# One transformer step on one core: everything behind the projections done for tokens 0-511, then for 512-1023

## The chip, the core and the metric

The kernel runs on one core of one Trainium2 chip. The core has five engines that run beside each other, each with its own queue of instructions taken in order: TensorE (PE, with its weight loads as PEld), VectorE (DVE), ScalarE (ACT), GpSimd (POOL) and SyncE (SP), which issues the DMAs. Waits between queues go by semaphores. The metric is the device time of one execution in microseconds.

## What is computed

One layer for 1024 new tokens of one sequence (D = 1024, the prompt) and 32 tokens of a second one that has 256 cached positions (the sample). Inputs and outputs are fp32.

```python
h = rms_norm(x, norm1_g) * (1 + sc1) + sh1
z = h @ w_in                                   # 1024 x 2884
q, k, v, qi, ki, wi, u, vg = jnp.split(z, SPLIT_POINTS, axis=-1)
...
score = jnp.einsum('bqhs,bqh->bqs', jax.nn.relu(s), w_idx)
score = jnp.where(mask[None], score, -jnp.inf)
top_val, top_idx = lax.top_k(score, topk)      # topk = 256, for the sample 72
...
p = jax.nn.softmax(logits, axis=-1)            # over the selected keys, 8 heads of 64
...
y = jnp.concatenate([attn.reshape(B, T, WIDTH_A), gm], axis=-1) @ w_out
x = x + g1 * y
h2 = rms_norm(x, norm2_g) * (1 + sc2) + sh2
x = x + g2 * (jnp.square(jax.nn.relu(h2 @ w_ff1)) @ w_ff2)   # 4096 hidden features
```

A query of the block b of 128 tokens sees at most the keys 0 to 128(b+1)-1. So blocks 0 and 1 need no selection, and a late block has more scores to search and more keys to attend to than an early one. `gm` is the gated unit, mixed within 128 positions.

## The kernel before

Every fp32 operand of a large product is split into two parts (a rounded one, and the difference), and a product is three passes (`PASSES`). A split of weights is a cast on ScalarE and a subtraction on VectorE or GpSimd (lines 183-184 for w_in, 756-757 for the rest).

**Front** (to about 475 us). Six groups of columns of z go through `zgroup` (line 303 has the matmul): first the indexer's columns, whose scores `score[b]` follow block by block, then q, the gated unit, k, v, each with its norms and rotations on VectorE and GpSimd. `ada` multiplies the conditioning vector. In between stand the searches of `find_top`: 31 bits of the k-th largest score are found one by one. On VectorE a bit is a trial value from GpSimd (line 551), one count for each block of the search (line 519), and two small operations (lines 554 and 555). On ScalarE a bit is a sum of signs (line 545) and two small operations on GpSimd (546 and 547). Search `tb` takes blocks 2 and 3, `tc` blocks 5, 4 and NB (the sample) on VectorE, `ta` block 7 and `td` block 6 on ScalarE. The four are generators, stepped round-robin:

```python
    while searches:
        searches = [f for f in searches if next(f, "end") is None]
```

This stands ahead of the last group (v) in the code; the framework's scheduler lists the instructions of each engine by a simulated time, so the steps spread over the whole front.

**Attention** (475 to 629 us), `attention(b)` for blocks 0, 2, 1, 3, 4, 5, NB, 6, 7. The queries are transposed (`qst`, line 351) and split (`qs`, 353-354). For each of 8 heads: scores of the keys into `lgp` (663), their masked minimum (664), Exp (665), scaling by the reciprocal on GpSimd (668), transposes `ppt` (675) and products with v (`pv`, 688). The keys stay in SBUF as `kst`. PSUM has 3 banks for lgp, 2 for ppt, 2 for pv, 1 for qst.

**Projection and perceptron** (629 to 1494 us). x, h2 and the hidden features lie with features on the partitions and all 1056 tokens (sample behind the prompt) in three chunks of 352 columns (`CW`). Weights are loaded and split once and stay while the three chunks pass. `wo` (812) adds to x; `norm2(c)` sums squares by a matmul with ones (783) and spreads the reciprocal root by another (789), among the wo and first f1 products of other chunks; `ff1` (831) and `ff2` (868) alternate over 16 groups of 256 hidden features, `gated` adds to x (749), `emit` transposes x back and stores.

## Time and profile before

| | us |
|---|---|
| three runs, median | 1496.52 |
| three runs, from and to | 1495.24 and 1497.37 |
| the profiled execution, first to last instruction | 1494.1 |
| front, to the first qst of attention | 474.8 |
| attention | 154 |
| projection with norm 2 | 112 |
| perceptron and end | 753 |

The profiled execution is shown by its span; the device times of the runs lie a little above it. The mean granted TensorE clock was 0.973 of full speed. A row of a view gives start and length or busy time in us; "idle before" is the time in which the engine did nothing ahead of a group's instructions, followed by what ended it.

### The profile page before, as it was taken

How to read it: one execution, taken by the hardware profiler on the slowest of the kernel's cores; microseconds unless marked ns; L12 is line 12 of the kernel's file. 1: busy time of each engine (PE TensorE's matmuls, PEld its weight loads, DVE VectorE, ACT ScalarE, POOL GpSimd, SP SyncE). 2: the span in 40 equal slices, each digit the busy share in tenths (PEclk: the TensorE clock that was granted, in tenths of full speed). 3: DMA queues.
4: the chain of work that ended last, by engine and by line, in shares of the span. 5: the costliest groups of instructions: out<-in, count | busy, mean ns of one | idle time of the engine just before them, and what ended most of it. 6: DMA issues, size and time to landing. Idle time of an engine off the chain costs nothing.

```text
span 1494.1 us, 24126 instructions
## 1 busy us (share of the span) xinstructions
PE 1408.7 (94%) x8952; PEld 1259.1 (84%) x8952; DVE 875.3 (59%) x2269; ACT 535.5 (36%) x1114; POOL 534.5 (36%) x816
## 2 busy tenths in 40 slices
PE   5789888988799999999999999999999999999998
PEld 1677666755557878899999999999999999999998
...
GB/s 361 58 54 45 65 60 47 68 172 240 147 217 112 62 69 65 58 91 97 29 58 43 43 43 55 45 43 43 54 46 43 44 50 50 43 43 43 56 30 88
DMA packets 127614, 115.00 MB, mean 77 GB/s; under 512 B 24181, under 2 KB 95305, under 8 KB 126985
## 3 DMA queue, kind: packets, MB, share of 16 engines
...
## 4 chain that ended last, share of the span: by engine, by line
PE 71%; DVE 19%; POOL 4%; issue 3%; ACT 1%; DMA 1%; SPq 0%; ACTq 0%; POOLq 0%; DVEq 0%
PE f L868 25%; PE f L831 25%; PE wo L812 6%; DVE tcjk L519 3%; PE lgp L663 3%; PE pv L688 3%; PE z L303 3%; PE ppt L675 2%; DVE tbjk L519 2%; PE xt L741 1%; DVE hf L244 1%; PE ada L143 1%; DVE rha L105 1%; DVE ssh L406 1%; PE qst L351 1%
## 5 line engine op out<-in xcount | busy, mean ns | idle before, releaser
L868 PE MATMUL f<-hid,w 128*128 128x352 f32 x2304 | 377.4, 323 | 0.0
L831 PE MATMUL f<-hh,w 128*128 128x352 f32 x2304 | 371.7, 322 | 0.0
L749 DVE SCALAR_TENSOR_TENSOR x<-f,mod,x 128x352 f32<-128x352 f32 (+1 forms) x480 | 222.1, 490 | 252.2 <-PE f L868 250.7
L868 PEld LDWEIGHTS f<-hid,w 128*128 128x128 f32 x2304 | 369.4, 188 | 0.5
L831 PEld LDWEIGHTS f<-hh,w 128*128 128x128 f32 x2304 | 369.2, 188 | 0.0
L303 PE MATMUL z<-wsp,h 128*128 128x512 f32 (+1 forms) x1152 | 288.5, 402 | 12.3 <-POOL wsp L184 5.2
L303 PEld LDWEIGHTS z<-wsp,h 128*128 128x128 f32 x1152 | 217.0, 200 | 71.8 <-issue 12.8
L836 POOL TENSOR_TENSOR rel<-rel 128x352 f32<-128x352 f32 x96 | 83.3, 869 | 513.0 <-ACT hid L835 513.0
L756 ACT CAST w<-w2r 128x1024 fp32r<-128x1024 f32 x32 | 33.6, 1051 | 280.8 <-PE f L868 269.7
L757 DVE TENSOR_TENSOR w<-w1r,w 128x1024 fp32r<-128x1024 f32 x32 | 39.7, 1244 | 137.1 <-ACT w L756 137.1
L833 ACT ACTIVATE rel<-f 128x352 f32<-128x352 f32 x96 | 44.3, 462 | 154.8 <-PE f L831 152.4
L837 POOL TENSOR_TENSOR hid<-rel,hid 128x352 fp32r<-128x352 f32 x96 | 92.7, 968 | 6.8
L668 POOL TENSOR_SCALAR lg<-lg,ast 128x128 f32<-128x128 f32 (+8 forms) x72 | 51.6, 719 | 92.8 <-DVE ast L667 58.4
L184 POOL TENSOR_TENSOR wsp<-wraw,wsp 128x512 fp32r<-128x512 f32 (+1 forms) x44 | 57.1, 1311 | 25.8 <-ACT wsp L183 25.5
L756 ACT CAST w<-w1r 128x1024 fp32r<-128x1024 f32 x32 | 33.5, 1049 | 85.8 <-PE f L831 73.3
L663 PE MATMUL lgp<-kst,qs 128*128 128x256 f32 (+1 forms) x336 | 60.3, 304 | 1.4 <-ACT qs L353 0.8
L757 DVE TENSOR_TENSOR w<-w2r,w 128x1024 fp32r<-128x1024 f32 x32 | 39.1, 1221 | 37.6 <-ACT w L756 37.6
L665 ACT ACTIVATE lg<-lg,ast 128x128 f32<-128x128 f32 (+8 forms) x72 | 53.9, 749 | 18.5 <-DVE ast L664 14.7
L519 DVE TENSOR_SCALAR_CACHE_REDUCE tcjk<-ya,tcsm 128x768 bf16<-128x768 int16 (+1 forms) x64 | 58.1, 940 | 2.1 <-POOL tcsm L551 1.7
L688 PE MATMUL pv<-pT,v 128*64 128x128 f32 (+2 forms) x624 | 57.0, 278 | 0.0
L749 DVE SCALAR_TENSOR_TENSOR x<-wo,mod,x 128x352 f32<-128x352 f32 (+2 forms) x32 | 15.0, 489 | 71.4 <-PE wo L812 71.2
L812 PE MATMUL wo<-attn,wo 128*128 128x352 f32 x288 | 52.7, 326 | 0.0
(354 smaller groups left out, 1874.9 us busy)
## 6 DMA issues: line engine op xcount, KB each, us to landing
wada<-in_w_ada_dram SPq DMA_DIRECT2D x24, 1024.0 KB, 6.8
...
x<-in_x_prompt_dram SPq DMA_DIRECT2D x4, 1024.0 KB, 9.8
...
```

The costliest lines, as they stand in the source:

```text
L303: nc.tensor.matmul(p[:m, :n], h[b][:, k, x, :], w[k][:, y, :], start=k == 0 and q == 0, stop=k == KT - 1 and q == 2)
L519: nc.vector.tensor_scalar(jk[:, :ncol[j]], src, val, None, op0=op, op1=OP.add, accum_out=cnt[:, j:j + 1])
L663: nc.tensor.matmul(ps[:m, d:d + kk.shape[1]], x, kk, start=q == 0, stop=q == 1)
L688: nc.tensor.matmul(ps[64 * j:64 * j + 64, :m], vv, pts[j][:w, k, :m], start=k == 0, stop=k == len(kts) - 1)
L749: nc.vector.scalar_tensor_tensor(y, ps[:, a:a + n], mod[:, 8 * part + k, s:s + 1], y, op0=OP.mult, op1=OP.add)
L756: nc.scalar.copy(ws[:, 0], raw)
L757: eng.tensor_tensor(ws[:, 1], raw, ws[:, 0].bitcast(F32), op=OP.subtract)
L812: nc.tensor.matmul(ps[:, :CW], ws[n][:, x, k, :], mix_at(k, c)[:, y, :], start=k == KO[0] and q == 0, stop=k == KO[-1] and q == 2)
L831: nc.tensor.matmul(ps[:, :CW], ws[n][:, x, k, :], h2_at(k, c)[:, y, :], start=k == 0 and q == 0, stop=k == KT - 1 and q == 2)
L836: nc.gpsimd.tensor_tensor(r, r, r, op=OP.mult)
L837: nc.gpsimd.tensor_tensor(hid[n][:, 1, c * CW:(c + 1) * CW], r, hi.bitcast(F32), op=OP.subtract)
L868: nc.tensor.matmul(ps[:, :CW], w[g][:, x, k, nn * P:(nn + 1) * P], hids[GH * g + k][:, y, c * CW:(c + 1) * CW], start=(g, k) == ks[0] and ...
```

## The change

The 1024 prompt tokens are split into two halves of 512 for all that follows the front. In the front, search `te` on VectorE takes blocks 2, 3 and NB. The searches of blocks 4 to 7 (`tc` with 5 and 4 on VectorE, `ta` and `td` on ScalarE) do only their first step there, the counts against zero; their bits are issued behind the last instructions of the first half's norm 2 (`late`). Then, in the order of the code: attention of blocks 0, 2, 1, 3 and NB; projection, norm 2 and perceptron of tokens 0-511 with the sample's; attention of blocks 4 to 7; projection, norm 2 and perceptron of tokens 512-1023.

The keys `kst` are also stored to DRAM (`ksd`) in the front and loaded again for the second half, with v, behind the last weights of the first half. In projection and perceptron x now lies with tokens on the partitions: `project` makes 128 tokens x 512 features (`pj`, line 742), for w_out and for w_ff2; f1 (line 886) makes 128 hidden features x 512 tokens. `gated` multiplies on VectorE (777) and adds on VectorE for w_out (778), on GpSimd for w_ff2. `norm2(b)` goes block by block: a square-sum on ScalarE, a reciprocal root on VectorE, two 1024-wide operations, eight transposes `h2t` (830), and casts and differences into `hh` (835). All weights of w_out, w_ff1 and w_ff2 are fetched and split twice. The sample's 32 tokens go through fp32 products of their own, with the token columns as the stationary side: `wot`, `f1t`, `f2t`, summed over four parts by `sum4` (`unfold`, `f1u`). The PSUM banks are two each for lgp and f1 (L), ppt, qst and the small ones (T), pv and the sample (V) and pj (A).

```diff
-CW = 352
-NCK = 3
+HT = 512
+HB = HT // P
...
+    ksd = drm.tile([P, NH, T], F32, name="ksd")
+    mrow = drm.tile([1, 4 * D], F32, name="mrow")
+    mix8 = cst.tile([P, KT, TS], F32, name="mix8")
...
+        if j < 4:
+            nc.sync.dma_start(ksd[:, :, 2 * j * P:2 * (j + 1) * P], kt.bitcast(F32))
...
-    searches = [find_top([2, 3], "tb", False, "JB"), find_top([5, 4, NB], "tc", False, "RL"), find_top([7], "ta", True, "JA"), find_top([6], "td", True, "JA")]
-    for f in searches:
...
+    def run(*fs):
+        fs = list(fs)
+        while fs:
+            fs = [f for f in fs if next(f, "end") is None]
...
+    top_e = find_top([2, 3, NB], "te", False, own)
+    ja = sc_b[:, 1408:1920].bitcast(I16)
+    top_l = [find_top([5, 4], "tc", False, kept(ya[:, 3328:4096])), find_top([7], "ta", True, kept(ja)), find_top([6], "td", True, kept(ja))]
+    for f in [top_e] + top_l:
         next(f)
...
-    while searches:
-        searches = [f for f in searches if next(f, "end") is None]
...
+    run(top_e)
     v_sb = {}
     kst, kstc = [], []
     zgroup(wv, 512, post_v, {0: (4, 0), 1: (1,), 2: (2, 5), 3: (3,)})
...
-    def attention(b):
...
+    def attention(wa, b, kst, v_sb, attn):
...
-                    ps = bank("lgp", "L", 3)
+                    ps = bank("lgp", "L")
...
-                    pt = bank("ppt", "T", 2)
+                    pt = bank("ppt", "T")
...
-    for b in (0, 2, 1, 3, 4, 5, NB, 6, 7):
-        attention(b)
...
+    def halves(wf, raw, view, eng):
+        out = []
+        for e in range(2):
+            x = view(raw, e)
+            ws = wf.tile([P, 2] + list(x.shape[1:]), F32R, name="ws", tag="W", bufs=6)
+            with tc.high_priority():
+                nc.scalar.copy(ws[:, 0], x)
+            eng.tensor_tensor(ws[:, 1], x, ws[:, 0].bitcast(F32), op=OP.subtract)
+            out.append(ws)
+        return out
...
+    def project(wf, w_rows, lhs, n5, nk, eng, tail=None):
+        ws = []
+        for g in range(nk // 4):
+            raw = raw_of(w_rows(g)[:, n5 * 512:(n5 + 1) * 512])
+            r4 = raw.rearrange("p (k c) -> p k c", k=4)
+            if tail:
+                tail(g, r4)
+            ws += halves(wf, r4, lambda r, e: r[:, 2 * e:2 * e + 2, :], eng)
+        for b in range(HB):
+            ps = bank("pj", "A")
+            for k in range(nk):
+                w = ws[k // 2][:, :, k % 2, :]
+                for q, (x, y) in enumerate(PASSES):
+                    nc.tensor.matmul(ps, lhs(k, b)[:, x, :], w[:, y, :], start=k == 0 and q == 0, stop=k == nk - 1 and q == 2)
+            yield b, ps
...
+        def gated(b, ps, n5, g, eng):
+            c = slice(n5 * 512, (n5 + 1) * 512)
+            y = x2[b // 2][:, b % 2, c]
+            t = tmp(wf, "gt")
+            nc.vector.tensor_tensor(t, ps, g[:, c], op=OP.mult)
+            eng.tensor_tensor(y, y, t, op=OP.add)
+            return y
...
+        def norm2(b):
+            x = x2[b // 2][:, b % 2, :]
+            ss = small(1, "ss2")
+            xn = rp.tile([P, 2048], F32, name="xn", tag="R", bufs=3)[:, :D]
+            nc.scalar.activation(xn, x, AF.Square, accum_out=ss)
+            nc.vector.tensor_scalar(ss, ss, 1.0 / D, EPS, op0=OP.mult, op1=OP.add)
+            r = rsqrt(ss, P, 1, "r2", nc.vector)
+            nc.vector.scalar_tensor_tensor(xn, x, r, a2b, op0=OP.mult, op1=OP.mult)
+            nc.vector.tensor_tensor(xn, xn, sh2, op=OP.add)
+            for c in range(0, KT, 4):
+                pt = tp("h2t")
+                for a in range(4):
+                    nc.tensor.transpose(pt[:, a * P:(a + 1) * P], xn[:, (c + a) * P:(c + a + 1) * P], ident)
+                for e in range(2):
+                    p2 = pt[:, e * 256:(e + 1) * 256].rearrange("p (k c) -> p k c", k=2)
+                    h = h2[c // 2 + e][:, :, :, b * P:(b + 1) * P]
+                    late["act"] = nc.scalar.copy(h[:, :, 0, :], p2).ins
+                    late["dve"] = nc.vector.tensor_tensor(h[:, :, 1, :], p2, h[:, :, 0, :].bitcast(F32), op=OP.subtract).ins
+        for n5 in range(2):
+            for b, ps in project(wf, wo_rows, mix, n5, 8, nc.vector, wo_tail(n5) if first else None):
+                gated(b, ps, n5, g1, nc.vector)
+                if n5 == 1:
+                    norm2(b)
...
+        def ff1(n2):
+            raw = raw_of(i["w_ff1"][0, :, n2 * 256:(n2 + 1) * 256]).rearrange("p (k c) -> p k c", k=KT)
...
+            ws = halves(wf, raw, lambda r, e: r[:, :, e * P:(e + 1) * P], nc.vector)
+            hid[n2] = slot([P, 2, 2, HT], F32R, f"hid{hf}{n2}")
+            for e in range(2):
+                ps = bank("f1", "L")
                 for k in range(KT):
                     for q, (x, y) in enumerate(PASSES):
-                        nc.tensor.matmul(ps[:, :CW], ws[n][:, x, k, :], h2_at(k, c)[:, y, :], start=k == 0 and q == 0, stop=k == KT - 1 and q == 2)
-                r = wr.tile([P, CW], F32, name="rel", tag="RE", bufs=3)
-                nc.scalar.activation(r, ps[:, :CW], AF.Relu)
-                hi = hid[n][:, 0, c * CW:(c + 1) * CW]
-                nc.scalar.activation(hi, r, AF.Square)
+                        nc.tensor.matmul(ps, ws[e][:, x, k, :], h2[k // 2][:, k % 2, y, :], start=k == 0 and q == 0, stop=k == KT - 1 and q == 2)
+                r = tmp(wf, "rel")
+                nc.scalar.activation(r, ps, AF.Relu)
+                h = hid[n2][:, e]
+                nc.scalar.activation(h[:, 0, :], r, AF.Square)
                 nc.gpsimd.tensor_tensor(r, r, r, op=OP.mult)
...
+            for n5 in range(2):
+                for b, ps in project(wf, lambda _: i["w_ff2"][0, g * 512:(g + 1) * 512, :], lhs, n5, 4, nc.vector, f2_tail(n5) if first else None):
+                    if g == NG - 1 and (n5, b) == (0, 0):
+                        last["raw"] = fetch[0]
+                    y = gated(b, ps, n5, g2, nc.gpsimd)
+                    if g == NG - 1:
+                        nc.sync.dma_start(o[0][0, t00 + b * P:t00 + (b + 1) * P, n5 * 512:(n5 + 1) * 512], y)
...
+    attn, gate = attend(0, (0, 2, 1, 3, NB), kst, v_sb)
+    gate = second_stage(0, attn, True, gate)
+    with tc.issue_after(late["dve"]), tc.issue_after(late["act"]):
+        run(*top_l)
+    kst2 = [slot([P, NH, 2 * P], F32R, f"ksr{j}") for j in range(4)]
+    v2 = [slot([P, 4, 512], F32, f"vr{j}") for j in range(2)]
+    with tc.issue_after(gate):
+        for j in range(4):
+            nc.sync.dma_start(kst2[j].bitcast(F32), ksd[:, :, 2 * j * P:2 * (j + 1) * P])
+        for j in range(2):
+            nc.sync.dma_start(v2[j], o[3][0, 0, 4 * j * P:4 * (j + 1) * P].rearrange("(k p) h d -> p k (h d)", p=P))
+    attn, gate = attend(1, (4, 5, 6, 7), kst2, v2)
+    second_stage(1, attn, False, gate)
```

The first place is TensorE at norm 2. Before, with wo the product with w_out, `ssq` and `r2b` the matmuls of norm 2, f the first perceptron products:

```order
L812 MATMUL wo<-attn_4918,wo 128x352 x3
L831 MATMUL f_8165<-hh_0_7760,w_8149 128x352 x9
L831 MATMUL f_8165<-hh_3_7773,w_8149 128x352 x9
L831 MATMUL f_8165<-hh_6_7786,w_8149 128x352 x4
L831 MATMUL f_8195<-hh_0_7760,w_8154 128x352 x4
L831 MATMUL f_8165<-hh_6_7786,w_8149 128x352 x2
L831 MATMUL f_8195<-hh_0_7760,w_8154 128x352 x5
L831 MATMUL f_8195<-hh_3_7773,w_8154 128x352 x9
L831 MATMUL f_8195<-hh_6_7786,w_8154 128x352 x4
L789 MATMUL r2b<-ident,r2y 128x128 x2
L789 MATMUL r2b<-ident,r2y 128x96
L783 MATMUL ssq<-ones,acc 128x1 x2
```

After, with `pj` the product with w_out of a block, and hh what norm 2 writes:

```order
L742 MATMUL pj<-ws,gm_5273 128x512 x6
L742 MATMUL pj<-ws,gm_5274 128x512 x6
L830 MATMUL h2t<-ident,xn 128x128 x8
L742 MATMUL pj<-ws,attn_4379 128x512 x6
L742 MATMUL pj<-ws,attn_4380 128x512 x6
L830 MATMUL h2t<-ident,xn 128x128 x24
L886 MATMUL f_5789<-hh_5301,ws 128x512
L886 MATMUL f_5819<-hh_5301,ws 128x512
L886 MATMUL f_5789<-hh_5301,ws 128x512 x5
L886 MATMUL f_5819<-hh_5301,ws 128x512 x5
L886 MATMUL f_5789<-hh_5302,ws 128x512
```

The matmuls of norm 2 stood among other products; the transposes of three blocks now stand in a row between the last product with w_out and the first f1.

The second place is VectorE there, after the change. `ws<-raw,ws` is a split of weights, xn and hh are norm 2 of the last block, `ya,tcsm` a count of search `tc`, big the sample's norm 2:

```order
L825 SCALAR_TENSOR_TENSOR xn<-x_5282,r2y,bc_5277 128x1024
L826 TENSOR_TENSOR xn<-xn,bc_5278 128x1024
L724 TENSOR_TENSOR ws<-raw,ws 128x1024 x2
L835 TENSOR_TENSOR hh_5301<-h2t,hh_5301 128x2x128
L835 TENSOR_TENSOR hh_5303<-h2t,hh_5303 128x2x128
L835 TENSOR_TENSOR hh_5302<-h2t,hh_5302 128x2x128
L835 TENSOR_TENSOR hh_5304<-h2t,hh_5304 128x2x128
L511 TENSOR_SCALAR ya,tcsm<-ya,tcsm 128x768
L531 TENSOR_SCALAR tasm<-tasm 128x1
L531 TENSOR_SCALAR tdsm<-tdsm 128x1
L511 TENSOR_SCALAR ya,tcsm<-ya,tcsm 128x640
L546 TENSOR_TENSOR tcsm<-tcsm 128x2
```

The counts began in the front before; now they follow the last hh, in the queue that also holds the splits of the next weights.

The third place is VectorE in a search. Before, in the front, with `vg` the gated unit:

```order
L519 TENSOR_SCALAR tbjk,tbsm<-ya,tbsm 128x512
L467 SCALAR_TENSOR_TENSOR vg<-vg,lst,sc_c 128x512
L519 TENSOR_SCALAR tcjk,tcsm<-ya,tcsm 128x768
L519 TENSOR_SCALAR tcjk,tcsm<-ya,tcsm 128x640
L467 SCALAR_TENSOR_TENSOR vg<-vg,lst,sc_c 128x512
L554 TENSOR_TENSOR tbsm<-tbsm 128x2
L519 TENSOR_SCALAR tcjk,tcsm<-sc_c,tcsm 128x288
L555 SCALAR_TENSOR_TENSOR tbsm<-tbsm 128x2
L554 TENSOR_TENSOR tcsm<-tcsm 128x3
L555 SCALAR_TENSOR_TENSOR tcsm<-tcsm 128x3
```

After, in the first half's perceptron, later in the same search; gt is the product of `gated`:

```order
L724 TENSOR_TENSOR ws<-raw,ws 128x1024
L511 TENSOR_SCALAR ya,tcsm<-ya,tcsm 128x640
L546 TENSOR_TENSOR tcsm<-tcsm 128x2
L547 SCALAR_TENSOR_TENSOR tcsm<-tcsm 128x2
L511 TENSOR_SCALAR ya,tcsm<-ya,tcsm 128x768
L724 TENSOR_TENSOR ws<-raw,ws 128x1024
L511 TENSOR_SCALAR ya,tcsm<-ya,tcsm 128x640
L558 CAST tamh<-tasm 128x1
L777 TENSOR_TENSOR gt<-pj,bc_5278 128x512
```

Two searches on VectorE alternated, with the work of z between; now one search goes on by itself, with splits and gate products between.

The fourth place is TensorE at a block's beginning in attention. Before, at block 6:

```order
L688 MATMUL pv<-pT,v_4770 64x128 x3
L663 MATMUL lgp<-kst_4802,qs 32x256 x2
L663 MATMUL lgp<-kstn,qs 32x32 x2
L351 MATMUL qst<-ident,qn 128x128 x4
L675 MATMUL ppt<-ident,lg 128x128 x4
L688 MATMUL pv<-pT,v_4603 64x128
L663 MATMUL lgp<-kst_4802,qs 32x256 x2
```

After, at block 5 of the second half:

```order
L699 MATMUL pv<-pT,vr_8842 64x128 x2
L340 MATMUL qst<-ident,qn 128x128 x8
L674 MATMUL lgp<-ksr_8837,qs 128x256
L674 MATMUL lgp<-ksr_8839,qs 128x256
L674 MATMUL lgp<-ksr_8837,qs 128x256
L674 MATMUL lgp<-ksr_8839,qs 128x256
L674 MATMUL lgp<-ksr_8838,qs 128x256 x2
```

The transposes of the queries stood among the previous block's ppt and pv; now they stand behind them.

## Rows read from the trace of the kernel before

**Rows 1.** The page: busy time of the engines; the chain that ended last, by line.

```profile
PE 1408.7 (94%) x8952; PEld 1259.1 (84%) x8952; DVE 875.3 (59%) x2269; ACT 535.5 (36%) x1114; POOL 534.5 (36%) x816
...
PE f L868 25%; PE f L831 25%; PE wo L812 6%; DVE tcjk L519 3%; PE lgp L663 3%; PE pv L688 3%; PE z L303 3%; PE ppt L675 2%; DVE tbjk L519 2%; PE xt L741 1%; DVE hf L244 1%; PE ada L143 1%; DVE rha L105 1%; DVE ssh L406 1%; PE qst L351 1%
```

**Rows 2.** Windows by stage: length; PE, PEld, DVE, ACT, POOL busy; PEclk; DMA; GB/s.

```profile
105.00:475.00 370.00, 321.97 (x1671) 232.78 (x1669) 347.73 (x1007) 187.07 (x392) 226.98 (x450) 0.93 0.36 114
475.00:629.00 154.00, 151.86 (x1377) 121.71 (x1375) 107.11 (x386) 97.38 (x261) 52.76 (x73) 1.00 0.26 72
629.00:741.00 112.00, 111.28 (x682) 103.98 (x682) 30.86 (x70) 32.21 (x63) 31.62 (x23) 1.00 0.27 77
741.00:1490.00 749.00, 748.90 (x4701) 747.58 (x4699) 319.09 (x615) 175.74 (x304) 177.16 (x193) 1.00 0.16 48
```

**Rows 3.** Groups on PE, 105 to 475 us: count, busy us, mean ns, idle before, releasers.

```profile
L303 PE MATMUL z<-wsp,h 128*128 128x512 f32 x960 | 251.3, 413 | 9.5 <-POOL wsp L184 3.8 <-DVE wsp L184 2.2 <-ACT u L482 1.5
...
L143 PE MATMUL ada<-wada,silu 128*32 128x512 f32 x128 | 21.2, 650 | 1.4 <-DMA wada<-in_w_ada_dram 1.4
```

**Rows 4.** Timeline of PE late in the front: start, length, instruction, count.

```profile
462.92 7.08 PE L303 MATMUL z<-wsp,h 128*128 128x512 f32 x30
...
394.34 1.90 PE L143 MATMUL ada<-wada,silu 128*32 128x512 f32 x16
```

**Rows 5.** The same, tiles tcsm (DVE, POOL), tasm and tdsm (DVE, ACT, POOL) alone.

```profile
105.00:475.00 370.00, 105.18 (x287) 8.73 (x30) 0.93 0.36 114
...
105.00:475.00 370.00, 12.77 (x21) 38.50 (x62) 23.19 (x62) 0.93 0.36 114
...
105.00:475.00 370.00, 10.11 (x21) 35.23 (x62) 22.67 (x62) 0.93 0.36 114
```

**Rows 6.** Groups by shape in attention, from 474 us on: ScalarE, VectorE, GpSimd.

```profile
L353 ACT CAST qs<-qst 128x512 fp32r<-128x512 f32 x16 | 9.3, 579 | 5.7 <-PE lgp L663 3.5 <-PE qst L351 2.2
...
L665 ACT ACTIVATE lg<-lg,ast 128x384 f32<-128x384 f32 x8 | 4.9, 618 | 2.7 <-DVE ast L664 2.7
...
L354 DVE TENSOR_TENSOR qs<-qst,qs 128x512 fp32r<-128x512 f32 x16 | 10.9, 684 | 3.5 <-ACT qs L353 3.4
...
L664 DVE CUSTOM_DVE_ANT_0 lg<-lgp,sc_c 128x384 f32<-128x384 f32 x8 | 4.2, 553 | 1.1 <-PE lgp L663 1.0
...
L678 DVE COPY pT<-ppt 128x256 f32<-128x256 f32 x8 | 3.4, 419 | 1.2 <-PE ppt L675 1.2
...
L668 POOL TENSOR_SCALAR lg<-lg,ast 128x384 f32<-128x384 f32 x8 | 4.6, 589 | 5.7 <-DVE ast L667 3.7 <-PE ppt L675 0.9 <-PE pv L688 0.6
```

**Rows 7.** Pieces of the chain, late front and perceptron: start us, length us, instruction, count.

```profile
463.17 6.84 PE z L303 x30
...
801.19 23.04 PE f L831 x144
```

**Rows 8.** The page: a split of weights; a DMA of 1 MB (KB, us to landing).

```profile
L757 DVE TENSOR_TENSOR w<-w1r,w 128x1024 fp32r<-128x1024 f32 x32 | 39.7, 1244 | 137.1 <-ACT w L756 137.1
...
wada<-in_w_ada_dram SPq DMA_DIRECT2D x24, 1024.0 KB, 6.8
```

**Rows 9.** Groups by shape on VectorE, 700 to 800 us: a small step of norm 2.

```profile
L105 DVE TENSOR_TENSOR r2a<-r2y 128x4 f32<-128x4 f32 x9 | 1.4, 157 | 0.1
```

**Rows 10.** Windows of 4 us in the front; columns as in rows 2.

```profile
400.00:404.00 4.00, 0.39 (x2) 0.00 (x0) 4.00 (x18) 0.00 (x0) 1.65 (x3) 0.78 0.00 0
404.00:408.00 4.00, 0.63 (x4) 0.50 (x4) 4.00 (x9) 0.00 (x0) 0.00 (x0) 0.50 0.56 162
408.00:412.00 4.00, 2.82 (x27) 1.20 (x28) 4.00 (x11) 2.40 (x5) 3.59 (x4) 0.50 0.91 256
412.00:416.00 4.00, 4.00 (x16) 1.78 (x15) 4.00 (x8) 0.00 (x0) 4.00 (x4) 0.52 0.92 320
```

**Rows 11.** Timeline of VectorE: start, length, instruction [idle before, what ended it].

```profile
324.48 1.01 DVE L519 TENSOR_SCALAR_CACHE_REDUCE tcjk<-ya,tcsm 128x768 bf16<-128x768 int16 x1 [0.55 <-POOL tcsm L551]
```

**Rows 12.** ScalarE at the Signs of line 545: idle us before and times, for td.

```profile
  POOL tdsm L547: 22.3, 14
```

388 lines of the change are left out of this document (190 added, 198 removed).

## The prediction

> **What bounds the kernel now.** I read the totals first, then the stages, then the chain, then single lines. TensorE shows 94% busy and heads the chain with its perceptron lines; VectorE shows 59%, and counts of the search (`tcjk`, `tbjk`) lead its part of the chain [rows 1]. The stages say where [rows 2]. From 741 to 1490 us (perceptron) TensorE has 748.9 of 749 us, at the full granted clock; from 629 to 741 (projection w_out) 111.3 of 112; in attention 151.9 of 154. There only TensorE work counts, and any hole in it is new time. From 105 to 475 us (the front: z, index scores, all searches) VectorE has 347.7 of 370 us. That stretch is bound by VectorE, whose share there is mostly counts of the top-score search.
>
> TensorE's 322 us in the front are not 322 us of work. A z record lasts 413 ns on average [rows 3], but 30 of them in a row take 7.08 us [rows 4], 0.236 us each. So z is 960 x 0.236 = 227 us; `ada` is 128 records, 16 in 1.90 us [rows 4], 15 us; all the rest shows 322.0 - 251.3 - 21.2 = 49 us, say 47 at full clock. Together 289 us of work in 370. The Trainium skill (Perfetto Trace Analysis, the note ahead of its first section) calls matmul busy time a bad metric, since matmuls are pipelined; the trace agrees, by 413 against 236 ns. By the busy time the front could shrink by 48 us at the very most, by the pace of the rows by 81.
>
> **The front.** Moved out are the searches of blocks 4 to 7. Their instructions on VectorE are 105.2 (`tc`) + 12.8 (`ta`) + 10.1 (`td`) us [rows 5]; block NB, 288 wide, stays and keeps about 17 of `tc`. VectorE's load falls to 348 - 128 + 17 = 237 us, ScalarE's by the 73.7 us of Signs in `ta` and `td`, GpSimd's by the 45.9 of these two. TensorE's 289 us become the longest. It won't run without holes: wsp splits, rotary chains and the reload of `kr` stay, 10 to 30 us of waits. At 91% use the stretch takes 316 us and ends at 421; at 97% it ends at 403, at 85% at 445. **Term: -54 us (-72 to -30).**
>
> **Attention.** The work is the same 154 us, now in two lots. Before, the `qst` of the next block stands among the `ppt` and `pv` of the one before; after, in both lots, it stands behind nearly all of them. From qst to the first ppt runs a chain: qs cast 0.58 and difference 0.68, lgp, the add-and-minimum 0.55, Exp 0.62, the scaling on GpSimd 0.59 [rows 6], about 4 us with the hand-overs for a block 384 wide, of which TensorE fills a part with further lgp. I take 2 us for each of nine blocks. Nothing hidden would be 4 us each. PSUM for lgp goes from 3 banks to 2, and qst shares two banks with ppt. **Term: +18 (+5 to +35).**
>
> **Projection and perceptron, TensorE's own work.** Before, 1494 - 629 = 865 us. The products now move 512 columns, 384 + 3072 matmuls; 352 columns took 0.160 us (144 in 23.04 [rows 7]), which makes 0.233 for 512; z with 512 took 0.228 in the chain (30 in 6.84 [rows 7]). I take 0.231: 3456 x 0.231 = 798. The 32 sample tokens leave these products and get fp32 products with 32 columns of the array: `wot` 16, `f2t` 64 of 512 columns, `f1t` 128 of 256. Four of 512 cost 0.95 us by `ada` (8 products are those 16 records in 1.90 [rows 4]): 3.8 + 15.2 + 15.2, with unfolding by `sum4` 39 us. `h2t` and the small transposes take 12; the transposes of x and y (16 + 13 us) are gone. Sum 849, **-16**. Weights are fetched and split twice; 48 GB/s and 319 us of VectorE in 749 [rows 2] leave room, so I put that at nothing where no search runs beside it.
>
> **Norm 2.** Before, statistics of a chunk lay among wo and f1 matmuls of other chunks and TensorE had no hole. Now nothing but `pj` of four blocks and `h2t` stands between, and the first f1 waits for hh of the last block. On VectorE a block needs two 512-wide operations for the gate (0.68 each, as qs [rows 6]), 11 dependent small ones (0.16 each [rows 9]), two 1024-wide (1.25 each, as a split [rows 8]), four 256-wide (0.42 each [rows 6]): 7.4 us, against 5.5 of pj. Ahead of the last hh stand four splits of 1.24, of weights of 1 MB whose buffers an earlier `xn` must free and which land 6.8 us after their issue [rows 8]. Counted from the end of the second product of the first block, VectorE reaches the last hh after 4 x 7.4 + 4 x 1.24 and some 3 of waiting for these weights, 38 us; TensorE has 17 of pj and 4.8 of h2t to fill them. So about 16 us idle in each half. **Term: +32 (+18 to +44).**
>
> **The clock after such holes.** In the front the granted clock was 0.50 from 404 to 412 us and 0.52 to 416, that is 1.2 instead of 2.4 GHz for some 12 us, behind a stretch in which TensorE was almost idle [rows 10]. TensorE was busy 7.5 of these 12 us and lost nearly 4; dense work all along would lose 6. I take 5 for each of the two holes: **+10 (0 to +16).** The Trainium skill (TensorE: Matmul & The Clock Gate, section on HAM oscillation) says that idle holes between bursts of matmuls let the clock fall, so that each burst starts cold; [rows 10] agree, and what that would make of every seam is rival 3.
>
> **The search beside the first half.** Behind the last hh come, on VectorE, the counts of 768 and 640 columns with their small steps, in one queue with the splits and the gate's products. That queue holds about 138 us until the search ends; a step waits 0.55 us for GpSimd where nothing lies between [rows 11], 18 times by the order, so 148 us, while TensorE has 139 us of work. TensorE falls behind by 10. Signs on ScalarE wait on GpSimd (22.3 us for `td` alone before [rows 12]) and hold up the Relus and casts queued behind them; GpSimd in turn squares hidden values between trial values. I add 3. Bounds: 4, and 55 if a third of the waits lands on the path. **Term: +13 (+4 to +55).** Three temporary buffers for gate products and Relus and two PSUM banks per use: +6 (0 to +25). Reload of keys and values, first weights, the end: +6.
>
> **Sum.** -54 + 18 - 16 + 32 + 10 + 13 + 6 + 6 = +15: span 1494.1 + 15 = 1509. Device times of the runs lie 1.1 to 3.3 us above that span, the median 2.4: **1511**.
>
> **Rivals.**
> 1. *The front's gain is kept.* TensorE is at 97% in the front, norm 2 costs 10 us each, the search hides under the matmuls, block seams cost 1 us: -72 + 9 - 16 + 20 + 5 + 4 + 3 + 6 = -41, about 1455; with the forecast's front 1473. For it: VectorE's 237 us leave 25% free, and GpSimd's and ScalarE's loads fall with it. Against: the order has nothing to fill the holes at norm 2.
> 2. *The search holds the perceptron.* Three engines wait for each other in order: a weight's split stands behind a count that waits for GpSimd, which waits for a Sign. If 55 us reach TensorE, 1511 + 42 = 1553. It decides from about a third of the waits on. For it: queue and TensorE are equal within 10 us. Against: weights are prefetched by two products' time.
> 3. *Cold restarts at all seams.* If the nine block seams too each bring a half-speed stretch at the 5 us above, 1511 + 45 = 1556. Against: attention before, with its small waits, kept clock 1.00 [rows 2].
> 4. *The change does not do what it says:* the front stays long because rotary chains and `kr` loads, not counts, end the waits; it gives back only 20 us, 1545. Against: counts head VectorE's part of the chain.
>
> **How the numbers follow.** Forecast 0.45 (1480 to 1545 by itself: the terms' ends seldom meet), rival 1 0.27, rival 2 0.17, rival 3 0.06, rival 4 0.05. Something like 0.2% is what a measurement of this kernel tells from no change, +-3 us. Faster: nearly all of rival 1 and an eighth of the forecast, 0.30; same 0.08; slower 0.62. The range reaches to the middle of rival 1 and past rivals 2 to 4: 1466 to 1556.
>
> **What would show it.** First qst of attention near 421 us (403 to 445); VectorE under 80% busy before it. Attention in two lots, together near 172 us. A hole of 14 to 20 us on TensorE between the last pj and the first f1 in both halves, and a granted clock near 0.5 behind it. VectorE almost full in the first 150 us of the first perceptron half, TensorE at about 93% there, and 98% in the rest. Wrong if the front ends past 445, if f1 follows pj without a hole, or if TensorE shows waits for VectorE's splits of over 30 us in the first half.

## The result, and the profile after

The changed kernel takes 1562.09 us (median of 4 runs, 1560.75 to 1563.95) against 1495.88 before: 1.044 times as long, 95% interval 1.0426 to 1.0455. The forecast was 1511, range 1466 to 1556: the sign was right, the size was not, and the time lies 6 us outside the range. The profiled execution's span is 1558.8 us, 64.7 more than before.

The page of the changed kernel, the lines that answer to [rows 1]:

```profile
PE 1425.2 (91%) x7623; PEld 1103.6 (71%) x7623; DVE 896.3 (57%) x2063; ACT 582.2 (37%) x1107; POOL 692.4 (44%) x866
...
PE pj L742 25%; PE f L886 18%; PE z L292 4%; PE pv L699 3%; PE lgp L674 3%; DVE jk L511 3%; DVE ya L511 3%; PE ppt L686 3%; DMA raw<-in_w_ff_dram 1%; DVE ws L724 1%; PE ada L132 1%; DVE lg L675 1%; PE f2t L905 1%; DVE hf L233 1%; PE qst L340 1%
```

VectorE's counts are still in the chain (`jk` and `ya`, line 511), at about the share they had; a load of weights and a split (`raw`, `ws`) are new in it.

The windows by stage, with the columns of [rows 2]: front, first attention lot, projection with norm 2, first perceptron half; second lot, projection, second half.

```profile
105.00:448.50 343.50, 305.75 (x1673) 226.70 (x1672) 258.72 (x759) 119.37 (x268) 171.03 (x289) 0.95 0.42 139
448.50:530.50 82.00, 74.76 (x520) 52.85 (x518) 43.79 (x171) 45.06 (x143) 20.83 (x40) 0.80 0.38 111
530.50:597.50 67.00, 54.45 (x260) 43.06 (x259) 44.00 (x97) 21.14 (x37) 0.21 (x1) 0.90 0.19 63
597.50:1028.00 430.50, 412.36 (x2013) 314.82 (x2012) 246.45 (x409) 176.77 (x286) 249.33 (x302) 0.97 0.31 102
1028.00:1140.00 112.00, 102.75 (x882) 82.32 (x880) 69.15 (x216) 57.96 (x122) 30.77 (x32) 0.96 0.25 72
1140.00:1201.40 61.40, 49.55 (x226) 40.81 (x225) 41.81 (x93) 19.84 (x33) 0.00 (x0) 0.89 0.21 69
1201.40:1553.60 352.20, 351.86 (x1537) 290.09 (x1536) 120.92 (x128) 99.72 (x127) 173.02 (x127) 0.99 0.28 92
```

| | before | after | difference | forecast |
|---|---|---|---|---|
| front, to the first qst | 474.8 | 448.5 | -26 | -54 |
| attention, one lot or two | 154 | 82 + 112 | +40 | +18 |
| projection, perceptron, end | 865 | 67 + 430.5 + 61.4 + 352.2 + 5.2 | +51 | +51 |

So the whole miss of 50 us lies in the first two lines. In the second half's perceptron TensorE is as dense as before (351.9 of 352.2 us busy, clock 0.99). Attention and the projections show lower clocks than [rows 2] has for the same work: 0.80 and 0.96 in the two lots, 0.90 and 0.89 in the projections, where it was 1.00.

**The front's end.** TensorE's timeline there (start, length, instruction, count, [idle before, what ended it]):

```profile
409.71 21.13 PE L292 MATMUL z<-wsp,h 128*128 128x512 f32 x92
...
432.15 0.94 PE L292 MATMUL z<-wsp,h 128*128 128x512 f32 x3
...
446.74 1.94 PE L328 MATMUL kst<-ident,kr 128*128 128x128 f32 x8 [10.36 <-DMA kr<-out_dram]
```

The last of z ends at 433 us. Then TensorE waits 10.4 us for the last keys (`kr`), which go to DRAM as rows and are loaded back for the transposes. SyncE's timeline says why they are late:

```profile
411.84 1.17 SPq L420 DMA_DIRECT2D out_dram<-v  x1
...
420.67 0.63 SPq L651 DMA_DIRECT2D qn<-qd  x1
...
422.83 0.42 SPq L437 DMA_DIRECT2D kr<-out_dram  x1
...
433.56 0.93 SPq L711 DMA_DIRECT2D raw<-in_w_out_dram  x2
...
435.71 0.52 SPq L443 DMA_DIRECT2D ksd<-kst  x1
...
436.41 3.36 SPq L437 DMA_DIRECT2D kr<-out_dram  x2
```

From 412 to 420.7 us SyncE's queue stands at the first load of q, which waits for a buffer; the loads of kr stand behind it. At 433.6 two weights of w_out and at 435.7 a store of keys go out, 3 MB in all, just ahead of the last kr. Before, products of z stood between the transposes of kr until 475 us, and kr was waited for once, 6.9 us.

**The clock.** Windows of 8 us in the first lot, columns as in [rows 2]:

```profile
440.00:448.00 8.00, 1.26 (x6) 1.29 (x7) 0.00 (x0) 0.08 (x1) 0.00 (x0) 0.50 0.81 287
448.00:456.00 8.00, 5.82 (x29) 4.84 (x27) 6.25 (x25) 7.30 (x20) 1.49 (x4) 0.71 0.41 119
456.00:464.00 8.00, 8.00 (x33) 4.97 (x33) 3.22 (x15) 3.42 (x15) 1.49 (x4) 0.50 1.26 225
464.00:472.00 8.00, 6.77 (x40) 5.94 (x39) 5.41 (x20) 4.91 (x14) 2.72 (x5) 0.78 0.42 136
472.00:480.00 8.00, 7.79 (x77) 6.09 (x77) 4.68 (x15) 4.15 (x13) 1.98 (x4) 1.00 0.00 0
...
504.00:512.00 8.00, 6.68 (x73) 4.42 (x72) 3.73 (x15) 3.05 (x11) 0.00 (x0) 0.99 0.46 151
512.00:520.00 8.00, 8.00 (x59) 5.44 (x59) 2.89 (x19) 4.38 (x21) 3.94 (x8) 0.50 0.12 46
520.00:528.00 8.00, 8.00 (x47) 4.83 (x50) 1.68 (x3) 1.72 (x9) 0.00 (x0) 0.50 0.00 0
```

Behind the hole the granted clock is 0.50, that is 1.2 GHz, well into the first blocks. Busy time times the missing clock, summed from 448 to 472 us, makes about 7 us. The clock falls to 0.50 again at about 512 us and stays there to 528, with TensorE busy all the time: there the 32-token block NB runs, alone until the sample's first products with w_out join it. Ahead of that fall stand two holes of 0.5 to 0.6 us.

**Norm 2.** TensorE between projection and perceptron in the first half:

```profile
577.34 2.99 PE L742 MATMUL pj<-ws,attn 128*128 128x512 f32 x12
...
581.94 0.63 PE L830 MATMUL h2t<-ident,xn 128*128 128x128 f32 x4 [1.18 <-DVE hh L835]
...
587.22 1.94 PE L830 MATMUL h2t<-ident,xn 128*128 128x128 f32 x8 [4.65 <-DVE r2a L96]
...
595.88 1.94 PE L830 MATMUL h2t<-ident,xn 128*128 128x128 f32 x8 [6.72 <-DVE xn L826]
...
597.47 4.97 PE L886 MATMUL f<-hh,ws 128*128 128x512 f32 x14
```

The holes are 1.2, 4.7 and 6.7 us, in the second half 0.5, 5.3 and 6.1: 24.4 in all. The first f1 come 0.36 us apart (14 in 4.97), against 0.23 later on. The first 8 us of the perceptron in each half:

```profile
597.50:605.50 8.00, 8.00 (x32) 6.27 (x30) 7.44 (x24) 6.87 (x12) 2.95 (x8) 0.81 0.43 134
...
1201.40:1209.40 8.00, 7.71 (x21) 5.60 (x21) 4.86 (x7) 2.91 (x5) 0.00 (x0) 0.58 0.87 292
```

**The search beside the first half.** What TensorE waits for there on gate products and splits (sum of us, times, longest):

```profile
PE pj L742 <- DVE gt L777: 7.0, 5, 3.7
...
PE pj L742 <- DVE ws L724: 2.2, 1, 2.2
```

### The profile page after: what moved, and what is told of

Its sections match the earlier page's. It is cut to its first block, busy times and chain, and to the rows that moved or that the text cites. A ratio compares the mean times of both kernels' runs of the same rounds, so it can differ in the third digit from the quotient of the medians.

```text
span 1558.8 us, 21057 instructions
## 1 busy us (share of the span) xinstructions
PE 1425.2 (91%) x7623; PEld 1103.6 (71%) x7623; DVE 896.3 (57%) x2063; ACT 582.2 (37%) x1107; POOL 692.4 (44%) x866
## 4 chain that ended last, share of the span: by engine, by line
PE 62%; DVE 22%; POOL 7%; issue 4%; DMA 3%; ACT 2%; POOLq 0%; SPq 0%; DVEq 0%; ACTq 0%
PE pj L742 25%; PE f L886 18%; PE z L292 4%; PE pv L699 3%; PE lgp L674 3%; DVE jk L511 3%; DVE ya L511 3%; PE ppt L686 3%; DMA raw<-in_w_ff_dram 1%; DVE ws L724 1%; PE ada L132 1%; DVE lg L675 1%; PE f2t L905 1%; DVE hf L233 1%; PE qst L340 1%
## 5 line engine op out<-in xcount | busy, mean ns | idle before, releaser
L742 PE MATMUL pj<-ws,hid 128*128 128x512 f32 x1536 | 370.2, 394 | 9.2 <-DVE gt L777 7.0
L886 PE MATMUL f<-hh,ws 128*128 128x512 f32 x1536 | 374.0, 396 | 2.9 <-DVE ws L724 1.9
L742 PEld LDWEIGHTS pj<-ws,hid 128*128 128x128 f32 x1536 | 289.9, 190 | 80.3 <-DVE gt L777 9.2
L886 PEld LDWEIGHTS f<-hh,ws 128*128 128x128 f32 x1536 | 290.7, 191 | 69.6 <-ACT rel L888 2.5
L724 DVE TENSOR_TENSOR ws<-raw,ws 128x1024 fp32r<-128x1024 f32 x144 | 184.2, 1285 | 234.5 <-ACT ws L723 234.2
L723 ACT CAST ws<-raw 128x1024 fp32r<-128x1024 f32 x144 | 150.0, 1051 | 415.0 <-PE pj L742 199.4
L778 POOL TENSOR_TENSOR x<-x,gt 128x512 f32<-128x512 f32 x128 | 189.4, 1481 | 205.5 <-DVE gt L777 205.0
L777 DVE TENSOR_TENSOR gt<-pj,bc 128x512 f32<-128x512 f32 x144 | 99.1, 688 | 192.5 <-PE pj L742 190.5
L891 POOL TENSOR_TENSOR rel<-rel 128x512 f32<-128x512 f32 x64 | 74.3, 1165 | 168.5 <-ACT hid L890 166.4
L892 POOL TENSOR_TENSOR hid<-rel,hid 128x512 fp32r<-128x512 f32 x64 | 83.9, 1315 | 2.7
```

The costliest lines, as they stand in the source:

```text
L723: nc.scalar.copy(ws[:, 0], x)
L724: eng.tensor_tensor(ws[:, 1], x, ws[:, 0].bitcast(F32), op=OP.subtract)
L742: nc.tensor.matmul(ps, lhs(k, b)[:, x, :], w[:, y, :], start=k == 0 and q == 0, stop=k == nk - 1 and q == 2)
L777: nc.vector.tensor_tensor(t, ps, g[:, c], op=OP.mult)
L778: eng.tensor_tensor(y, y, t, op=OP.add)
L886: nc.tensor.matmul(ps, ws[e][:, x, k, :], h2[k // 2][:, k % 2, y, :], start=k == 0 and q == 0, stop=k == KT - 1 and q == 2)
```

## Experiments

What the runs were to test: that the front lost to transfers and their queue on SyncE, attention to the shared PSUM bank of qst and to half clock, the perceptron to full queues. Each run's own theory A and rival stand with it. All figures by stage are from the profiled executions, the times are medians of two runs where nothing else is said. A stage whose code is the same still varies: the front takes 338 to 350 us (343.5 in the changed kernel) and the first lot 78 to 83 (82.0 there).

**What the move of the search gives and takes.** Two kernels: without the late searches behind norm 2 (no_late), and with all searches in the front (all_front).

```diff
     with tc.issue_after(late["dve"]), tc.issue_after(late["act"]):
-        run(*top_l)
+        pass
```

> The searches of blocks 4 to 7 are left out behind norm 2 (their first step in the front stays), so these blocks attend with wrong masks; all other work stays. It prices the search in the first half's perceptron. By the prediction's term (13 us, 4 to 55) and the 14 us of waits that the trace of the changed kernel shows between 597 and 760 us: 1562 - 13 - 5 of half clock = 1542 to 1550. Rival (the search holds the perceptron through more than the waits shown): below 1530.

1530.55 us, far below the expected range and at the rival's bound. The first perceptron half falls from 430.5 to 407.8:

```profile
588.00:995.80 407.80, 404.66 (x2012) 310.32 (x2012) 133.48 (x161) 108.17 (x162) 178.92 (x144) 0.99 0.33 108
```

VectorE's 246 us there become 133, TensorE's idle time 18 us becomes 3, the clock 0.99. The search costs 23 us, 8 more than TensorE's idle time shows: its busy time falls by 8 too, with the clock. The other 9 of the 31.5 lie in the front (5) and the first lot (4), whose code is the same. The lot's 4 are within what unchanged lots differ by. In the front the scheduler put the w_out weights behind the last kr here, and the last wait for kr is 5.4 us instead of 10.4:

```profile
437.11 0.86 SPq L437 DMA_DIRECT2D kr<-out_dram  x2
438.00 1.02 SPq L711 DMA_DIRECT2D raw<-in_w_out_dram  x2
...
441.19 1.09 PE L328 MATMUL kst<-ident,kr 128*128 128x128 f32 x4 [5.44 <-DMA kr<-out_dram]
```

```diff
-    run(top_e)
+    run(top_e, *top_l)
...
-        run(*top_l)
+        pass
```

> All searches run in the front again, the late ones beside the early one; the halves stay as in the changed kernel. It tells what the moved search alone gives. Theory A (the move gives the front 26 us and costs the perceptron 15 to 20): front ends near 475, first perceptron half 15 to 20 us shorter, time 1566 to 1574. Rival (the front's gain is much smaller than the search's cost in the perceptron, so that the move itself is the mistake): below 1555.

1571.27 us, theory A. The front ends at 482.7, 34 us later, and the first half takes 407.8 as without the search. VectorE is back at what [rows 2] shows for the front, 348 us:

```profile
105.00:482.70 377.70, 323.76 (x1697) 235.28 (x1696) 348.68 (x1014) 187.70 (x398) 230.03 (x447) 0.91 0.38 122
```

The move by itself gains 9 us. So the halves alone, with the search where it was, cost 1571 - 1496 = 75: that is where the kernel lost.

**The order on SyncE.** First (kr_first), stores of keys and w_out weights behind the last kr (`krl[0]` is its load):

```diff
-        if j < 4:
-            nc.sync.dma_start(ksd[:, :, 2 * j * P:2 * (j + 1) * P], kt.bitcast(F32))
...
+    with tc.issue_after(krl[0]):
+        for j in range(4):
+            nc.sync.dma_start(ksd[:, :, 2 * j * P:2 * (j + 1) * P], kst[j].bitcast(F32))
...
+        with tc.issue_after(krl[0]):
+            fetch[0] = nc.sync.dma_start(r.rearrange("p (k c) -> p k c", k=src.shape[0] // P), src.rearrange("(k p) c -> p k c", p=P)).ins
```

> The four stores of keys to DRAM and the first two loads of w_out weights are issued behind the last load of keys to be transposed (kr); everything else as in the changed kernel. Theory A (the front's end is lost to transfers: in the changed kernel 3 MB of stores and weights are issued within 3 us ahead of the last kr load, which then takes 10 us, and TensorE restarts at half clock): the 10.4 us wait of kst for kr falls to 4 us or less, first qst of attention near 440 instead of 448.5, less half clock in the first block, in all 8 to 14 us less than the changed kernel, 1548 to 1554. Rival (the last kr load waits for its buffer, held by v rows on their way to DRAM, and the wait stays or moves to the first weights of w_out, which now come 10 us later): within 4 us of 1562.

1561.22 us, the rival. TensorE's last wait for kr, and its wait for q (in all, times, longest):

```profile
443.43 1.94 PE L328 MATMUL kst<-ident,kr 128*128 128x128 f32 x8 [2.83 <-DMA kr<-out_dram]
...
PE qst L340 <- DMA qn<-qd: 7.7, 1, 7.7
```

The wait for kr fell from 10.4 to 2.8 us, so the 3 MB ahead of it had been most of it. But now 6 MB, the four stores and two weights, stood ahead of the loads of q, and block 2 waited 7.7 us for them. The wait had only moved. Second (sp_order), q behind kr as well, and the large transfers behind the last load of q (`gate`):

```diff
+        with tc.issue_after(krl[0]):
+            fetched = nc.sync.dma_start(qn[:m].rearrange("p (a s c) -> p a s c", a=NH, s=2), twice(heads(qd[t0:t0 + m]), m, NH)).ins
...
+    krl[0] = gate
+    with tc.issue_after(gate):
+        for j in range(4):
+            nc.sync.dma_start(ksd[:, :, 2 * j * P:2 * (j + 1) * P], kst[j].bitcast(F32))
```

> The loads of q are issued behind the last load of keys (kr), and the stores of keys and the first w_out weights behind the loads of q; the rest as in the changed kernel. In the changed kernel SyncE sits from 412 to 420.7 us at the first load of q, which waits for a buffer, with two kr loads queued behind it; then 3 MB of stores and weights go out ahead of the last kr. Theory A (the front's lost 27 us are these two queueings and the half clock behind them): kst waits for kr under 6 us in all at the front's end, first qst near 438 and full clock in block 0, time 1545 to 1553. Rival (kr comes as late for another reason, such as v rows holding its buffer; or the weights of w_out now come late): above 1557.

1549.05 us: 13 less, in theory A's range, which set out to explain 27. TensorE at the front's end:

```profile
430.01 1.03 PE L328 MATMUL kst<-ident,kr 128*128 128x128 f32 x8
...
436.18 1.94 PE L328 MATMUL kst<-ident,kr 128*128 128x128 f32 x8 [5.14 <-DMA kr<-out_dram]
...
439.29 1.94 PE L340 MATMUL qst<-ident,qn 128*128 128x128 f32 x8 [1.18 <-DMA qn<-qd]
```

The wait is 5.1 + 1.2 us instead of 10.4 and attention begins at 439.3, 9 us earlier, but half clock still follows, against theory A. Not all of the 9 need be the order: three kernels below with the same order begin at 445 to 446. Of the runs that leave the front's groups and searches as they are, the front takes 334 to 341 us where the last wait for kr is 5 us or less, and 343 to 350 where it is 10 to 11. Third (k_early), the group of k ahead of the gated unit, on its own:

```diff
+    zgroup(zweights(CK, 512), 512, post_k)
     zgroup(zweights(CG, 512), 512, post_vg)
-    zgroup(zweights(CU, 512), 512, post_u)
-    wn_ = zweights(CK, 512)
+    wn_ = zweights(CU, 512)
...
-    zgroup(wn_, 512, post_k)
+    zgroup(wn_, 512, post_u)
```

> The column group of k is computed second, ahead of the gated unit, in place of fifth, just ahead of v; the rest as in the changed kernel. The keys then reach DRAM long before they are loaded back for the transposes. Theory A (the front's lost time is the way of the last keys through DRAM, which has no z left to hide it): the waits of kst for kr, 17.1 us in two holes, nearly go, and with them the half clock behind them; first qst at 425 to 432, time 1535 to 1545. Rival (the loads of kr stand in SyncE's queue behind the first load of q and behind v's stores whatever the group's place): kst waits above 8 us, time above 1553.

1565.15 us. The waits for kr fell from 17.1 to 6.0, as theory A had it, yet the time is the rival's, and the front got 10 us longer:

```profile
PE z L292 <- DVE ssh L398: 16.1, 3, 10.2
...
PE kst L328 <- DMA kr<-out_dram: 6.0, 1, 6.0
```

Another wait, z for the reduction over heads on VectorE (`ssh`), took their place, 16.1 us in place of 5.0. The front's rest is thus no single transfer.

**qst in other banks than ppt (qst_bank).**

```diff
-        return bank(name, "T")
+        return bank(name, "A" if name == "qst" else "T")
```

> The transposes of queries (qst) get the two PSUM banks of pj, idle in attention, in place of the two that they share with ppt; nothing else changes. Theory A (the shared bank keeps the next block's qst behind the last ppt of the block before, so each block starts with an empty TensorE): the two lots of attention, 82 and 110 us in the changed kernel, fall by 10 to 20 us together, time 1542 to 1552. Rival (the blocks' starts cost little, and attention's extra time is the half clock behind the wait for keys and in the 32-token block): the qst move earlier but the lots fall by less than 5 us, time above 1557.

1540.66 us, 21 less: theory A, 1 us below its range. The first lot and the qst of block NB, which stood at 506 us before:

```profile
449.90:519.10 69.20, 67.35 (x520) 49.57 (x518) 42.98 (x171) 43.74 (x143) 20.88 (x40) 0.83 0.46 132
...
476.37 0.67 PE L340 MATMUL qst<-ident,qn 32*128 32x32 f32 x8
```

The first lot falls from 82.0 to 69.2 us, the second from 112 to 110.3, the first perceptron half by 6, since the second lot's first qst now goes ahead of the half's last transposes. TensorE's idle time in the first lot falls from 7.2 to 1.9 us. So the late qst was not the order of the code but the rotation of two PSUM buffers among qst and ppt. NB's products now run among those of other blocks as well, so that this gain and NB's price below are not apart.

**Block NB.** Left out (no_nb), and in the middle (nb_mid):

```diff
+    nc.gpsimd.memset(mix8[:, 0:4, :], 0.0)
-    attn, gate = attend(0, (0, 2, 1, 3, NB), kst, v_sb)
+    attn, gate = attend(0, (0, 2, 1, 3), kst, v_sb)
```

> Attention of the 32-token block NB is left out (its rows are zero); the rest as in the changed kernel. The trace of the changed kernel shows it alone at the end of the first lot, from 511 to 530 us, at a granted clock of 0.50. Theory A (alone, this block costs its whole chain at half clock, 16 to 20 us, where in the kernel before it lay among block 6's work and cost some 5): first lot 62 to 66 us in place of 82, time 1542 to 1547. Rival (part of that time is the wait for w_out weights and gated rows and the half clock then falls on the projection): time above 1552.

1534.42 us, 8 below theory A; the first lot takes 63.0, as theory A had it, so NB costs 19 us there, or 15 against the lots of 78. As in no_late, the w_out weights stand behind the last kr here and the front is 4 us shorter, which is not NB's work.

```diff
-    attn, gate = attend(0, (0, 2, 1, 3, NB), kst, v_sb)
+    attn, gate = attend(0, (0, 2, NB, 1, 3), kst, v_sb)
```

> Block NB is attended third in the first lot, ahead of blocks 1 and 3, in place of last; the rest as in the changed kernel, qst still in the bank of ppt. Leaving NB out took 19 us from the lot. Theory A (its price is its place: last, with only the wait for its own chain and the half clock behind it): 8 to 14 us less, time 1548 to 1554. Rival (with the shared bank the blocks follow each other as before, and NB costs the same chain and clock in any place): within 4 us of 1562.

1557.32 us, the first lot 79.0, within what an unchanged lot takes: between the two, nearer to the rival. The windows of 8 us where NB now runs:

```profile
480.00:488.00 8.00, 7.25 (x80) 4.78 (x77) 4.83 (x27) 5.82 (x23) 3.30 (x7) 1.00 0.56 161
488.00:496.00 8.00, 8.00 (x60) 6.73 (x59) 1.37 (x5) 2.59 (x13) 0.65 (x2) 0.56 0.34 123
496.00:504.00 8.00, 6.81 (x33) 5.00 (x31) 5.34 (x28) 5.28 (x19) 3.75 (x8) 0.59 0.67 246
504.00:512.00 8.00, 7.20 (x52) 4.91 (x51) 4.52 (x12) 3.43 (x10) 0.00 (x0) 1.00 0.18 49
```

The drop of the clock went with the block. It came at about 489 us; TensorE's last gap ahead of it, 0.2 us, ended at 483.4. The same place together with the changes of sp_order and qst_bank above and of spread below (best_nb):

> The kernel with the order on SyncE, qst in the banks of pj and the spread search (1527), and NB third. Theory A: with qst free to go ahead, NB's small products mix with those of blocks 1 and 3, and the lot falls from 68 to 60 or less: 1516 to 1521. Rival (in that kernel NB lay already among others; or it lowers the clock of its neighbours): 1525 to 1531.

1529.46 us against 1526.94: the rival. The lot took 75.3 in place of 68.2, and the clock of 0.50 (488 to 496 us) now fell on products of NB's neighbours too, with TensorE busy all the time from 472 on. So an earlier place in the first lot did not lower NB's price, and here it cost 7 us in the lot. A place among a late block's products, where NB lay before, was not tried:

```profile
560.00:590.00 30.00, 30.00 (x281) 24.07 (x280) 20.36 (x77) 17.49 (x55) 10.41 (x14) 1.00 0.23 84
```

There, before the change, the clock stayed at 1.00.

**The sample's products in the perceptron left out (no_tail).**

```diff
-            if first:
+            if False:
                 p8 = bank("f1t", "V")
...
-nc.vector, f2_tail(n5) if first else None):
+nc.vector, None):
```

> The sample's 32-column products in the perceptron (f1t, f1u, f2t) are left out; the sample's projection, norm and last sums stay. By the prediction these products are 30.4 us and some 4 of unfolding on TensorE; the trace of the changed kernel shows 52 us of busy time on them. Theory A (they cost what the pace of ada says): 1562 - 34 = 1528, within 4. Rival (as seen by their share of busy time, or with temporary buffers and waits that they bring into the search's stretch): below 1520.

1520.5 us, between theory and rival, from two runs of 1515.54 and 1525.46 that do not settle which. The first half falls by 41 us to 389.5; TensorE's busy time there by 51 (412.4 to 361.6), its idle time rises from 18 to 28: part of what these products took had covered the search's lag.

**Norm 2's holes.** Work handed to GpSimd (pool_norm), and below it the chain left out (no_norm):

```diff
-                gated(b, ps, n5, g1, nc.vector)
+                gated(b, ps, n5, g1, nc.vector if n5 else nc.gpsimd)
...
-            ws = halves(wf, raw, lambda r, e: r[:, :, e * P:(e + 1) * P], nc.vector)
+            ws = halves(wf, raw, lambda r, e: r[:, :, e * P:(e + 1) * P], nc.vector if n2 > 1 else nc.gpsimd)
```

> The differences of the first two w_ff1 weights of each half and the additions to x of the first half of the w_out columns go from VectorE to GpSimd, which is idle there (0.2 of 67 us). Theory A (norm 2's hole is VectorE's queue): the waits of h2t, 24.4 us in both halves, fall by 4 x 1.24 + 4 x 0.68 = 7.7 us a half at most, since only the splits stand in the stretch: 8 to 12 us in all, time 1550 to 1554. Rival (the hole is the chain of each block's norm, square-sum, root, two wide operations, and the queue is not what fills it): within 4 us of 1562.

1564.03 us: no gain, the rival's time; the projections take 67.2 and 61.5 us as in the changed kernel. The rival's reason is not all of it. Two of the wide additions of norm 2 in this kernel, then GpSimd:

```profile
584.47 1.22 DVE L826 TENSOR_TENSOR xn<-xn,bc 128x1024 f32<-128x1024 f32 x1
...
591.85 2.70 DVE L826 TENSOR_TENSOR xn<-xn,bc 128x1024 f32<-128x1024 f32 x1
```

```profile
587.83 5.63 POOL L724 TENSOR_TENSOR ws<-raw,ws 128x1024 fp32r<-128x1024 f32 x2 [13.60 <-ACT ws L723]
```

While GpSimd runs the splits (2.8 us each), VectorE's addition takes 2.70 us in place of the 1.22 that it also takes in the changed kernel. The Trainium skill (GPSIMD Engine Reference, section 1, Specifications) says that GpSimd's SBUF interfaces are shared with VectorE; these rows agree.

```diff
-            nc.vector.tensor_scalar(ss, ss, 1.0 / D, EPS, op0=OP.mult, op1=OP.add)
-            r = rsqrt(ss, P, 1, "r2", nc.vector)
-            nc.vector.scalar_tensor_tensor(xn, x, r, a2b, op0=OP.mult, op1=OP.mult)
-            nc.vector.tensor_tensor(xn, xn, sh2, op=OP.add)
...
-                    nc.tensor.transpose(pt[:, a * P:(a + 1) * P], xn[:, (c + a) * P:(c + a + 1) * P], ident)
+                    nc.tensor.transpose(pt[:, a * P:(a + 1) * P], x[:, (c + a) * P:(c + a + 1) * P], ident)
```

> In norm 2 the root and the two wide operations are left out, and h2t transposes x itself, so the perceptron works on rows that are not normalised; the square-sum and all else stay. It prices the two holes between projection and perceptron. The trace of the changed kernel shows 24 us of waits at h2t and a granted clock of 0.79 to 0.85 around them. Theory A (the hole is these operations in VectorE's queue, and behind it comes a stretch at half clock): 24 + 6 to 10 us, time 1528 to 1534. Rival (h2t then waits for the first weights or the sample's norm in its place): above 1540.

1542.22 us, just in the rival's range. The projections fall by 9.3 and 8.7 us, 18 in place of 24; h2t then waits 5.4 us for hh, and f1 4.4 in all for the casts of weights. So the holes of 24.4 us become 9.8: the norm's chain is about 15 of them, 18 with the clock, and the rest moved to other waits. The first 8 us of the perceptron, which the expectation has at a clock of 0.79 to 0.85, are at 0.81 and 0.58 in the changed kernel, as shown above.

**Spreading the search, and the mends together.**

```diff
-        run(*top_l)
+        top_l = [f for f in top_l if next(f, "end") is None]
+    for a in [m for n, m in enumerate(marks[8:]) if n % 8 in (0, 2, 4, 5, 7)]:
+        with tc.issue_after(a):
+            top_l = [f for f in top_l if next(f, "end") is None]
```

(`marks` holds the gate products of the first half; this is spread.)

> The steps of the late searches are spread over the first half's perceptron, one behind each of five of eight products of a group of w_ff2, in place of all as early as they go; the rest as in the changed kernel. Leaving the searches out took 23 us from the first perceptron half. Theory A (that price is queues filled for 150 us, a step's waits standing ahead of splits and gate products, and spread out most of it hides under the matmuls): first perceptron half 412 to 418 in place of 430.5, time 1544 to 1551. Rival (each step costs its part wherever it stands, since splits, gate products and Relus wait behind it all the same): within 5 us of 1562.

1553.11 us (1548.72 and 1557.49), between theory and rival; the first half takes 419.1 in place of 430.5, by the profile of the faster run. So spreading takes back about half of the search's 23 us, and half stays with the work.

The changes of sp_order and qst_bank together (sp_qst):

> The two edits that each gained: loads of q behind those of keys and the large stores and w_out weights behind the loads of q, and qst in the banks of pj. Theory A (one shortens the front, the other the first attention lot): they add up, 1562 - 13 - 21 = 1528, within 5. Rival (both live on the same hole at the first block, so that the second gives little): above 1536.

1536.97 us: the two gave 25 of 34, the rival is nearer. The front ended at 445.0 here, not at 439.3: beside the other bank the order on SyncE gained 4 us (1540.66 to 1536.97).

The same with that of k_early (combo):

> The former kernel with the column group of k computed second as well. Theory A: the gain of the early keys comes on top, less what the order on SyncE already took: 1515 to 1522, the structure of halves then still 20 us behind the kernel before, by the sample's own products, the two holes at norm 2 and the search beside the first half. Rival (no further gain, 1528).

1548.87 us, against both: early keys cost 12 us against sp_qst, and the front is 12 longer. Alone they made the front 10 us longer too, but the time only 3.

sp_order, qst_bank and spread together (sp_qst_spread):

> The order of loads and stores on SyncE, qst in the banks of pj, and the spread search together. Theory A: 1537 as measured for the first two, less what the spreading gives by its own run (10 to 18): 1519 to 1527, still slower than the kernel before. Rival (no gain by spreading): 1535 to 1539.

1526.94 us (1526.13 to 1529.38), 1.0203 times the kernel before, interval 1.0186 to 1.022: the best of these versions, theory A at its upper end. The first half takes 416.9 us, the first lot 68.2:

```profile
446.40:514.60 68.20, 66.91 (x519) 49.27 (x519) 41.39 (x169) 42.78 (x141) 21.05 (x40) 0.83 0.62 207
```

It takes back 35 of the 66 us. No version here beats the kernel before.

## Why the prediction missed

**The front: wrong.** The step is "At 91% use the stretch takes 316 us": it allows 27 us for all that is not work. No run speaks against the 289 us of work, and most of VectorE's fall came (348 to 259, forecast 237). But the stretch took 343.5, a use of 84%: 289 of work, 38 of idle time, and 16 in which TensorE was busy beyond that work. For these 16 nothing had been set, though the kernel before showed 322 - 289 = 33 of the same kind. By windows of 4 us, busy time times the missing clock, low clock is about 8 of the 16 and was 19 of the 33; the rest stays open. Of the idle time 17.1 us were the keys' way through DRAM, against 6.9 before. I had named the reload of `kr` among the waits that stay, and not asked which work covers it: z, which now ends first. The queue that the new stores and early loads stand in on SyncE was not followed. kr_first shows that these transfers make most of the last wait, and the orders that mend it shorten the front by about 5 to 9 us; k_early shows that with the keys early other waits take their place. The prediction's own sign of being wrong, a front past 445 us, came with 448.5. What the other 18 us or more of the 28 come from one by one stays open.

**Attention: wrong.** "I take 2 us for each of nine blocks" and its bound of 35 both failed: +40. The chain at a block's start was seen, and that qst shares banks with ppt was named, but priced with the rest at 2 us a block (qst_bank: 15 us of both lots, 21 of the kernel). Missing were NB, 15 to 19 us in the first lot (before it lay among block 6, at clock 1.00), and the half clock behind the front's hole, about 7. These three overlap and need not add up. Rival 3 had half clock behind the seams, for all alike, at 0.06; NB's half clock came without a hole of that size.

**Projection and perceptron: right in sum, +51.** TensorE's own work: 352.2 us for a half's 1536 products (forecast 355). Sample: 41 against 34, from a run pair 10 us apart. Holes: 24.4 against 32, about 15 of it the named chain. Clock behind them: 0.81 and 0.58 in the first 8 us, about 5 us in all (8.0 x 0.19 + 7.7 x 0.42) against 10. Search: 22.7 against 13, inside its bounds, by waits and low clock of rival 2's kind at less than half of its 55 us. The errors cancel, which is luck as far as the sum goes; the terms for buffers, reload and end (6 and 6) were not measured apart.

**The rest.** Rival 1 fell with the front. Rival 4 was nearer than the forecast there: it gave the front 20 us, by `kr` loads among others, and 26 came, with `kr` the longest wait. But its premise that the counts are not what holds the front fell with all_front, whose front is 34 us longer with them; the move does what it says and is worth 9 us after its cost. The times of rivals 2 and 3, 1553 and 1556, are near the result for other reasons.
